# Constants multiplied into a free PSUM bank wherever the order's plan has TensorE idle

## The chip, the cores and the metric

The kernel runs on one core of a Trainium2 chip. The metric is the device time of one execution in microseconds. Before the change three runs took 1372.06, 1376.14 and 1377.72 us, a median of 1376.14 us. A fourth execution was profiled; everything said of the inside of the kernel is from it.

## The reference

One step of a streaming encoder of two layers, in fp32. There are 512 frames of a new stream (prompt) and 64 frames of a running one (sample), with D = 1024. Per layer, cut to what matters:

```python
proj = x @ w_in                      # q | k | v | conv_a | conv_gate
q, k = rope(q), rope(k)              # 8 sub heads of 64
s = q @ k.T * HEAD_DIM ** -0.5       # chunk mask in the prompt; cached keys in the sample
a = softmax(s)[0] - lam * softmax(s)[1]          # differential attention, 4 heads
o = rms_norm(a @ v) * sub_g * (1 - lam_init)
u = conv_a * sigmoid(conv_gate)
c = silu(layer_norm(depthwise_conv31(u)))
x = layer_norm(ALPHA * x + concat(o, c) @ w_out)
x = layer_norm(ALPHA * x + square(relu(x @ w_ff1)) @ w_ff2)
```

It returns x of both streams and the new keys, values and convolution states.

## The kernel before, in words

All activations lie transposed, features on the 128 partitions and the 576 frames (512 + 64) along the free dimension, in two column groups of 288 (`GS`). Eight tiles `r` of 128 features hold x. Every large product is split: an fp32 operand becomes a high half (rounded to fp32r: `wh`, and the first tile of a pair `x`) and a low half (what is left: `wl`, and the second of the pair), and `tri` multiplies three times, high by high, high by low, low by high (lines 734 to 736). The halves are made on the core: a weight block of 128 x 1024 comes by DMA into `raw`, ScalarE casts the high half (L891), VectorE or GpSimd subtracts for the low half (L894); some low halves are made by a DMA that adds (L878). The feed-forward products use a Strassen form on 2 x 2 blocks, whose sums of weight blocks and of results add work on VectorE.

The stages of a layer are: the input projection, mixed with attention and the depthwise convolution (31 taps, most of them fused multiply-adds on VectorE into PSUM, L1337); the output projection; a LayerNorm; the two feed-forward products; a second LayerNorm. In a LayerNorm the mean over features is a product with a constant matrix `ones_d` of 1/1024 (L1029 and L1034), VectorE subtracts it (L1052), ScalarE squares (L1058), GpSimd adds the squares (L1064), TensorE sums them with products that are one column wide (L1006), VectorE makes the reciprocal root (L959 to L987), TensorE spreads it (L1125), and VectorE multiplies (L1133).

PSUM is four one-bank tiles `b` and two two-bank tiles `sc`. In the rows of the order below the four `b` are called b_114 to b_117, since buffers are numbered through.

What sets the order is a planner (`Sched`). Each operation is a node with a cost in us per engine that may run it, the nodes it depends on, buffers that it acquires and releases, and a priority. `Sched.run` goes through a modelled time: an engine that is free takes the first available node by priority whose buffers are free; the instruction is issued at that moment, so each engine's program is the order in which the plan started its nodes. The plan has a model of TensorE's clock: it sums TensorE's activity in windows of 4096/1200 us (`HAMW`, `act`), and in a window after too little of it (`HAML`, `HAMH`) it doubles TensorE's costs (`cold`). Priorities and choices stand in tables of numbers, one per stage (`PHASES`); the change leaves them alone. Each engine executes its own program strictly as planned; waits on other engines are semaphores, added where tiles are written and read. So if an operation is late on the chip, what stands behind it on its engine is late too.

The lines touched are the class `Sched` (its `run`, and what decides when an engine is idle) and one helper beside `tri`.

Of the kernel before, what the change touches and what calls it, by code (L numbers as in the profile page):

```python
# [119 lines left out]
HAMW, HAML, HAMH = 4096 / 1200, 0.45, 0.9  # L120
# [13 lines left out]
GAPP = [int(i) for i in "".split()]  # L134
HB = 0
PRE = 20
PD = 0.1
DM, GD, GDL = 0.0, 0.88, 6.5
PRP, PRS = 889.2, -10.4
# [372 lines left out]
class Sched:  # L512
# [4 lines left out]
    def __init__(self, caps):  # L517
        self.free, self.nodes = {t: list(range(k)) for t, k in caps.items()}, []
        self.free["half"] = []
        self.now = None  # L520

    def room(self, tag):
# [35 lines left out]
    def delay(a, b):  # L558
# [3 lines left out]
            return 0.0  # L562
        return 0.2 if "P" in (a, b) else 0.13

    def run(self, engines):
        for n in self.nodes:
            n.left = len(n.deps)
# [8 lines left out]
        for n in reversed(order):  # L576
            n.at = min(n.eng.values()) + n.lat + max((s.at for s in n.succ), default=0.0)
            n.pri += n.at
        avail = sorted((n for n in self.nodes if n.left == 0), key=lambda n: -n.pri)
        busy = {e: 0.0 for e in engines}  # L580
        ends, t, count = [], 0.0, 0
        act, cold, win = {}, True, 0
        port = 0.0
        while count < len(self.nodes):
            again = True
            while again:
                again = False
                for e in engines:
                    if busy[e] > t + 1e-9:
                        continue  # L590
                    for i, n in enumerate(avail):
                        if n.ready > t + 1e-9 or e not in n.eng:
                            continue
                        c = n.eng[e]
# [23 lines left out]
                            n.got.setdefault(a, []).append(self.get(a))  # L618
                        self.now = {a: list(k) for a, k in n.got.items()}
                        del avail[i]  # L620
                        busy[e], n.at = t + c, t
                        if shared:
                            port = t + c
                        if e == "P":
                            a = t
                            while a < t + c - 1e-9:
                                k = int(a / HAMW + 1e-9)
                                b = min(t + c, (k + 1) * HAMW)
                                act[k] = act.get(k, 0.0) + b - a
                                a = b  # L630
# [15 lines left out]
                        break  # L646
            times = [b for b in (*busy.values(), port) if b > t] + [n.ready for n in avail if n.ready > t] + [x for x, _ in ends]
            assert times, ("stuck", count, len(self.nodes), self.free, [(n.acq, n.fn) for n in avail[:10]])
            t = min(times)
            for x, rel in [y for y in ends if y[0] <= t + 1e-9]:  # L650
                for a, n in rel:
# [10 lines left out]
def tile_hymba_step(ctx: ExitStack, tc: tile.TileContext, xT, wu, ck, cconv, par, cst,  # L662
# [29 lines left out]
    tl = {}  # L692
# [27 lines left out]
    sch = Sched(CAPS)  # L720
# [12 lines left out]
    def tri(o, wh, wl, xh, xl, start, stop):  # L733
        TE.matmul(o, wh, xh, start=start, stop=False)  # L734
        TE.matmul(o, wh, xl, start=False, stop=False)  # L735
        TE.matmul(o, wl, xh, start=False, stop=stop)  # L736

    def bank():
        return take("b")
# [1689 lines left out]
```

## Time and profile before

| what | value |
|---|---|
| median of three runs | 1376.14 us |
| the profiled execution | 1375.67 us |
| its span, first to last instruction | 1373.9 us |
| TensorE busy | 1308.0 us, 95% of the span |
| VectorE busy | 1078.1 us, 78% |
| ScalarE busy | 705.1 us, 51% |
| GpSimd busy | 302.3 us, 22% |
| mean granted TensorE clock | 0.977 of full speed |

How to read it: PE is TensorE's matmuls, PEld its weight loads (which overlap), DVE VectorE, ACT ScalarE, POOL GpSimd, SP the queue that starts most transfers. A row of a timeline has the start, the duration, the engine, the source line, the operation, output and inputs by name, and in brackets how long the engine idled before and what ended that. A row of stretches has the time from and to, its length, then busy time and number of instructions per engine in the order of its first row, then the granted clock, the share of the DMA engines and GB/s. Matmuls are pipelined: the end of one is modelled and overlaps the next, so the price of one is read from the distance of two starts. Before the first record of the clock, at 10.2 us, it is shown as 1.00. An fp32 product that isn't split stands as two records.

### The profile page before, as it was taken

The numbers are of one execution on the slowest core, as the hardware profiler recorded it, in microseconds if no ns is written. First come the engines' busy times: TensorE is split into PE (matmuls) and PEld (weight loads), VectorE is DVE, ScalarE is ACT, GpSimd is POOL, SyncE is SP. The second block draws the span as 40 slices with busy tenths as digits, with TensorE's granted clock in tenths as the row PEclk, the third lists the DMA queues.
The fourth block names the chain that finished last, engine by engine and source line by source line (L and its number), as shares of the span: only waits on it lengthen the run. The fifth ranks groups of instructions, "written<-read, shape, count | busy, mean of one in ns | idle before, by whom it ended". The sixth has DMA issues, their size and how long they took to land.

```text
span 1373.9 us, 24858 instructions
## 1 busy us (share of the span) xinstructions
PE 1308.0 (95%) x9518; PEld 1264.1 (92%) x9518; DVE 1078.1 (78%) x2206; ACT 705.1 (51%) x1413; POOL 302.3 (22%) x292
## 2 busy tenths in 40 slices
PE   8989989979999999999999999899989999999997
PEld 7878879979899999999998988798889999999996
DVE  5899998777888887878658999868677676767737
ACT  5766677265444444434156657754654443434424
POOL 0456620150000000000144885223400000000013
PEclk9999989989999999999999999899999999999998
DMA  6635533334465645554345444454234343435262
GB/s 220 162 94 140 122 117 106 93 130 156 144 211 165 208 168 192 185 167 139 102 158 204 160 152 121 129 135 118 64 79 117 112 108 108 124 80 144 70 152 69
DMA packets 70102, 186.38 MB, mean 136 GB/s; under 512 B 10848, under 2 KB 16608, under 8 KB 69984
## 3 DMA queue, kind: packets, MB, share of 16 engines
q1 hardware_dynamic: 63504, 161.20, 34.9%
q0 software_dynamic: 6480, 23.60, 10.4%
q8 instruction: 75, 1.23, 0.4%
q14 instruction: 43, 0.35, 0.1%
HBM read 154.11 MB, written 30.65 MB: 134 GB/s over the span
## 4 chain that ended last, share of the span: by engine, by line
PE 72%; DVE 18%; issue 3%; DMA 2%; ACT 2%; POOL 2%; SPq 0%; ACTq 0%; DVEq 0%; POOLq 0%
PE b L734 21%; PE b L735 21%; PE b L736 21%; DVE sc L1337 8%; DMA raw<-in_wu_dram 2%; PE sc L734 1%; PE b L1006 1%; POOL sq L1064 1%; PE sc L736 1%; PE b L1568 1%; PE sc L735 1%; DVE nm L1486 1%; DVE P L1530 1%; DMA wl<-in_wu_dram 1%; PE b L1611 1%
## 5 line engine op out<-in xcount | busy, mean ns | idle before, releaser
L734 PE MATMUL b<-x,wh 128*128 128x288 f32 x1356 | 416.2, 307 | 6.6 <-ACT wh L891 4.0
L736 PE MATMUL b<-x,wl 128*128 128x288 f32 x1356 | 406.1, 299 | 7.0 <-DVE wl L894 4.8
L735 PE MATMUL b<-x,wh 128*128 128x288 f32 x1356 | 406.5, 300 | 1.7 <-DVE x L1215 1.1
L734 PE MATMUL b<-a,wh 128*128 128x288 f32 x1088 | 325.0, 299 | 0.2 <-ACT x L731 0.2
L735 PE MATMUL b<-a,wh 128*128 128x288 f32 x1088 | 321.3, 295 | 0.0
L736 PE MATMUL b<-a,wl 128*128 128x288 f32 x1088 | 321.0, 295 | 0.0
L734 PEld LDWEIGHTS b<-x,wh 128*128 128x128 f32 x1356 | 260.5, 192 | 13.5 <-ACT wh L891 4.0
L736 PEld LDWEIGHTS b<-x,wl 128*128 128x128 f32 x1356 | 260.2, 192 | 8.2 <-DVE wl L894 5.3
L735 PEld LDWEIGHTS b<-x,wh 128*128 128x128 f32 x1356 | 260.6, 192 | 4.0 <-DVE x L1215 2.5
L734 PEld LDWEIGHTS b<-a,wh 128*128 128x128 f32 x1088 | 205.1, 188 | 2.0 <-issue 0.6
L735 PEld LDWEIGHTS b<-a,wh 128*128 128x128 f32 x1088 | 205.4, 189 | 0.5
L736 PEld LDWEIGHTS b<-a,wl 128*128 128x128 f32 x1088 | 205.1, 188 | 0.0
L2273 DVE TENSOR_TENSOR r<-r,b 128x288 f32<-128x288 f32 x192 | 85.7, 450 | 87.6 <-PE b L736 87.3
L1337 DVE SCALAR_TENSOR_TENSOR sc<-ub,par,sc 128x606 f32<-128x606 f32 x160 | 136.2, 851 | 4.2
L878 POOL DMA_DIRECT2D wl<-in_wu_dram x45 | 39.2, 871 | 446.8 <-ACT wl L875 387.6
L1064 POOL TENSOR_TENSOR sq<-sq,sq 128x288 f32<-128x288 f32 x40 | 35.7, 910 | 416.1 <-ACT sq L1058 415.5
L1325 POOL TENSOR_TENSOR r<-r,prod 128x606 f32<-128x606 f32 x72 | 113.7, 1580 | 54.8 <-ACT prod L1322 31.0
L891 ACT CAST wh<-raw 128x1024 fp32r<-128x1024 f32 (+1 forms) x73 | 71.4, 979 | 71.2 <-PE b L735 52.3
L2056 ACT CAST wh<-ckv 128x512 fp32r<-128x512 f32 x104 | 64.1, 620 | 76.7 <-PE b L735 61.2
L894 DVE TENSOR_TENSOR wl<-raw,wh 128x1024 fp32r<-128x1024 f32 (+1 forms) x73 | 84.5, 1161 | 22.3 <-ACT wh L891 21.7
L1884 DVE TENSOR_TENSOR wl<-ckv,wh 128x512 fp32r<-128x512 f32 x104 | 71.1, 685 | 6.0 <-ACT wh L2056 5.8
L875 ACT ACTIVATE wl<-raw 128x1024 fp32r<-128x1024 f32 x45 | 47.7, 1060 | 44.2 <-PE b L736 25.5
(320 smaller groups left out, 2409.9 us busy)
## 6 DMA issues: line engine op xcount, KB each, us to landing
raw<-in_wu_dram SPq DMA_DIRECT2D x110, 512.0 KB, 4.6
wl<-in_wu_dram POOLq DMA_DIRECT2D x45, 512.0 KB, 7.2
wscr<-cs SPq DMA_DIRECT2D x80, 256.0 KB, 2.0
ckv<-in_wu_dram SPq DMA_DIRECT2D x26, 512.0 KB, 3.6
ah<-in_wu_dram SPq DMA_DIRECT2D x26, 512.0 KB, 4.4
cs<-in_wu_dram SPq DMA_DIRECT2D x40, 256.0 KB, 2.8
wh<-wscr SPq DMA_DIRECT2D x20, 512.0 KB, 3.3
wl<-wscr SPq DMA_DIRECT2D x20, 512.0 KB, 4.4
```

Source lines behind the costliest of these rows:

```text
L734: TE.matmul(o, wh, xh, start=start, stop=False)
L735: TE.matmul(o, wh, xl, start=False, stop=False)
L736: TE.matmul(o, wl, xh, start=False, stop=stop)
L875: S.activation(wt["lo"], wt["raw"], AF.Copy, scale=-1.0)
L891: S.copy(wt["hi"][:, c], wt["raw"][:, c])
L894: e.tensor_tensor(wt["lo"][:, c], wt["raw"][:, c], wt["hi"][:, c].bitcast(F32), op=ALU.subtract)
L1064: e.tensor_tensor(q[a]["t"], q[a]["t"], q[b]["t"], op=ALU.add)
L1325: GP.tensor_tensor(cc[t], cc[t], st[j], op=ALU.add)
L1337: V.scalar_tensor_tensor(st["a0"], win(j), w, st["a0"], op0=ALU.mult, op1=ALU.add)
L1884: e.tensor_tensor(o, a, b, op=ALU.subtract)
L2056: S.copy(tl["wh"][box["i"]][:, off:off + n], src())
L2273: V.tensor_tensor(rr, rr, bk(), op=ALU.add)
```

## The change

When the plan has nothing that TensorE can start, and a bank `b` is free, and real TensorE work is still left, the planner now inserts a node of 0.23 us on TensorE: a product of the constant tile `ones_d` (128 x 128, fp32) with itself into the first 128 columns of the free bank. Nobody reads the result; the bank stays free in the plan, and whoever takes it next starts its accumulation anew. The node counts as activity in the plan's clock model and occupies TensorE in modelled time, so a real node that becomes available meanwhile is started up to 0.23 us later, and every later choice of the plan may differ. The limit `FT * FW` = 2.2 us on activity within the last 2.0 us is never reached. The name *keeper* is used below for such a product; the program has 129 of them.

```diff
--- before.py
+++ after.py
@@ -134,6 +134,7 @@
 GAPP = [int(i) for i in "".split()]
 HB = 0
 PRE = 20
+FT, FW, FC = 1.1, 2.0, 0.23
 PD = 0.1
 DM, GD, GDL = 0.0, 0.88, 6.5
 PRP, PRS = 889.2, -10.4
@@ -517,6 +518,7 @@
     def __init__(self, caps):
         self.free, self.nodes = {t: list(range(k)) for t, k in caps.items()}, []
         self.free["half"] = []
+        self.keep, self.recent, self.plast = None, [], None
         self.now = None
 
     def room(self, tag):
@@ -561,6 +563,19 @@
         if "N" in (a, b):
             return 0.0
         return 0.2 if "P" in (a, b) else 0.13
+
+    def spare(self, t, busy, avail):
+
+
+        if not FT or self.keep is None or busy > t + 1e-9 or not self.free["b"] or not self.left_p():
+            return False
+        return sum(min(b, t) - max(a, t - FW) for a, b in self.recent if b > t - FW) < FT * FW
+
+    def left_p(self):
+
+        while self.plast and self.plast[-1].at is not None and self.plast[-1] in self.done:
+            self.plast.pop()
+        return bool(self.plast)
 
     def run(self, engines):
         for n in self.nodes:
@@ -577,6 +592,7 @@
             n.at = min(n.eng.values()) + n.lat + max((s.at for s in n.succ), default=0.0)
             n.pri += n.at
         avail = sorted((n for n in self.nodes if n.left == 0), key=lambda n: -n.pri)
+        self.plast, self.done = [n for n in self.nodes if "P" in n.eng], set()
         busy = {e: 0.0 for e in engines}
         ends, t, count = [], 0.0, 0
         act, cold, win = {}, True, 0
@@ -618,10 +634,13 @@
                             n.got.setdefault(a, []).append(self.get(a))
                         self.now = {a: list(k) for a, k in n.got.items()}
                         del avail[i]
+                        if e == "P":
+                            self.done.add(n)
                         busy[e], n.at = t + c, t
                         if shared:
                             port = t + c
                         if e == "P":
+                            self.recent = [x for x in self.recent if x[1] > t - FW] + [(t, t + c)]
                             a = t
                             while a < t + c - 1e-9:
                                 k = int(a / HAMW + 1e-9)
@@ -646,6 +665,20 @@
                         break
             times = [b for b in (*busy.values(), port) if b > t] + [n.ready for n in avail if n.ready > t] + [x for x, _ in ends]
             assert times, ("stuck", count, len(self.nodes), self.free, [(n.acq, n.fn) for n in avail[:10]])
+            if self.spare(t, busy["P"], avail):
+                n = self.op({"P": FC}, lambda e: self.keep(e, self.free["b"][0]))
+                n.left, n.at, self.now = 0, t, {}
+                busy["P"] = t + FC
+                self.recent = [x for x in self.recent if x[1] > t - FW] + [(t, t + FC)]
+                a = t
+                while a < t + FC - 1e-9:
+                    k = int(a / HAMW + 1e-9)
+                    b = min(t + FC, (k + 1) * HAMW)
+                    act[k] = act.get(k, 0.0) + b - a
+                    a = b
+                n.fn(engines["P"])
+                count += 1
+                continue
             t = min(times)
             for x, rel in [y for y in ends if y[0] <= t + 1e-9]:
                 for a, n in rel:
@@ -734,6 +767,10 @@
         TE.matmul(o, wh, xh, start=start, stop=False)
         TE.matmul(o, wh, xl, start=False, stop=False)
         TE.matmul(o, wl, xh, start=False, stop=stop)
+
+    def keep(e, k):
+        TE.matmul(tl["b"][k][:, :128], ones_d, ones_d, start=True, stop=True)
+    sch.keep = keep
 
     def bank():
         return take("b")
```

Line numbers behind the diff's places are 33 to 37 higher in the changed kernel: `tri` is at lines 767 to 769 there, and the keeper at 772.

**At the start**, TensorE's program was, from its first product on (accumulating in b_114):

```order
L734 MATMUL b_114<-x_171,wh_83 128x288
L735 MATMUL b_114<-x_172,wh_83 128x288
L736 MATMUL b_114<-x_171,wl_87 128x288
L734 MATMUL b_114<-x_173,wh_83 128x288
L735 MATMUL b_114<-x_174,wh_83 128x288
L736 MATMUL b_114<-x_173,wl_87 128x288
```

Now it is, with keepers (L772) into the bank of the first product and then into the next free one:

```order
L772 MATMUL b_114<-ones_d 128x128 x19
L767 MATMUL b_114<-x_171,wh_83 128x288
L768 MATMUL b_114<-x_172,wh_83 128x288
L769 MATMUL b_114<-x_171,wl_87 128x288
L772 MATMUL b_115<-ones_d 128x128
L767 MATMUL b_114<-x_173,wh_83 128x288
L768 MATMUL b_114<-x_174,wh_83 128x288
L769 MATMUL b_114<-x_173,wl_87 128x288
L772 MATMUL b_115<-ones_d 128x128 x2
```

Nineteen keepers stand ahead of all real work, and single ones or pairs between the triples of products.

**Late in layer 0's attention**, TensorE's program was, around the transposes of the probabilities P (L1539), scores of the sample (`ckh`, `ckl`: cached keys), P times V (L1568) and transposes of v (L1410):

```order
L736 MATMUL sc_118<-ckh_2061,a_1832 128x512
L734 MATMUL b_114<-a_1908,a_1831 128x64
L735 MATMUL b_114<-a_1909,a_1831 128x64
L736 MATMUL b_114<-a_1908,a_1832 128x64
L1568 MATMUL b_115<-ah_99,a_1808 128x256
L1568 MATMUL b_115<-ah_99,a_1808 128x128
L1539 MATMUL b_117<-ident,P_2088 128x128 x3
L1410 MATMUL sc_119<-ident,r_98 128x128 x5
L1725 MATMUL sc_119<-dg_2127,ones_68 128x288 x2
```

Where these operations meet now (L1576, L1605 and L1447 are the same three lines), the program reads:

```order
L772 MATMUL b_117<-ones_d 128x128 x2
L1576 MATMUL b_117<-ident,P_2056 128x128
L772 MATMUL b_114<-ones_d 128x128 x2
L1576 MATMUL b_114<-ident,P_2083 128x128 x2
L772 MATMUL b_115<-ones_d 128x128 x7
L1605 MATMUL b_115<-ah_99,a_1841 128x256
L1605 MATMUL b_115<-ah_99,a_1841 128x128
L772 MATMUL b_117<-ones_d 128x128 x2
L1447 MATMUL sc_119<-ident,r_91 128x128 x5
L772 MATMUL b_117<-ones_d 128x128 x4
L767 MATMUL sc_118<-ckh_2092,a_1871 128x512
```

Seventeen keepers in five runs stand between ten real products; the scores with cached keys, which stood ahead of the first P times V, follow behind.

**In layer 0's first LayerNorm**, on VectorE, from the last multiplication of the first column group (L1133) through the subtractions of the mean in the second (L1052) to the low halves of the first feed-forward weights (L894):

```order
L1133 TENSOR_TENSOR r_91<-r_91,b_114 128x288
L1052 TENSOR_TENSOR r_97<-r_97,b_115 128x288
L1052 TENSOR_TENSOR r_95<-r_95,b_115 128x288
L1052 TENSOR_TENSOR r_98<-r_98,b_115 128x288
L1052 TENSOR_TENSOR r_94<-r_94,b_115 128x288
L1052 TENSOR_TENSOR r_92<-r_92,b_115 128x288
L819 TENSOR_TENSOR cs_3006<-cs_3006 128x512
L1052 TENSOR_TENSOR r_93<-r_93,b_115 128x288
L1052 TENSOR_TENSOR r_96<-r_96,b_115 128x288
L1052 TENSOR_TENSOR r_91<-r_91,b_115 128x288
L894 TENSOR_TENSOR wl_87<-raw_81,wh_83 128x1024
L894 TENSOR_TENSOR wl_88<-raw_82,wh_84 128x1024
```

Now (L1170, L1089 and L931 are the same lines):

```order
L1170 TENSOR_TENSOR r_98<-r_98,b_116 128x288
L931 TENSOR_TENSOR wl_87<-raw_82,wh_83 128x1024
L1089 TENSOR_TENSOR r_97<-r_97,b_114 128x288
L1089 TENSOR_TENSOR r_91<-r_91,b_114 128x288
L1089 TENSOR_TENSOR r_96<-r_96,b_114 128x288
L1089 TENSOR_TENSOR r_93<-r_93,b_114 128x288
L1089 TENSOR_TENSOR r_92<-r_92,b_114 128x288
L1089 TENSOR_TENSOR r_94<-r_94,b_114 128x288
L1089 TENSOR_TENSOR r_95<-r_95,b_114 128x288
L1089 TENSOR_TENSOR r_98<-r_98,b_114 128x288
L856 TENSOR_TENSOR cs_3056<-cs_3056 128x512
L931 TENSOR_TENSOR wl_88<-raw_81,wh_84 128x1024
```

The low half of the first weight (wl_87) moved from behind the eight subtractions to ahead of them.

On TensorE, at the same place, from the mean of the second column group (L1029, L1034) to the sums of squares (L1006), `x` being the operands of the feed-forward that the first group has already given:

```order
L734 MATMUL b_117<-x_2987,wh_83 128x288
L735 MATMUL b_117<-x_2988,wh_83 128x288
L736 MATMUL b_117<-x_2987,wl_87 128x288
L734 MATMUL b_117<-x_3001,wh_83 128x288
L735 MATMUL b_117<-x_3002,wh_83 128x288
L736 MATMUL b_117<-x_3001,wl_87 128x288
L734 MATMUL b_116<-x_2987,wh_84 128x288
L735 MATMUL b_116<-x_2988,wh_84 128x288
L736 MATMUL b_116<-x_2987,wl_88 128x288
L734 MATMUL b_116<-x_3001,wh_84 128x288
L735 MATMUL b_116<-x_3002,wh_84 128x288
L736 MATMUL b_116<-x_3001,wl_88 128x288
```

Directly behind these twelve products came L1006. Now the piece begins, with keepers around the mean (L1066, L1071):

```order
L772 MATMUL b_114<-ones_d 128x128 x8
L1066 MATMUL b_114<-sg_108,ones_d 128x288
L1071 MATMUL b_114<-r_98,ones_d 128x288
L772 MATMUL b_115<-ones_d 128x128 x7
L767 MATMUL b_115<-x_3036,wh_83 128x288
L768 MATMUL b_115<-x_3037,wh_83 128x288
L769 MATMUL b_115<-x_3036,wl_87 128x288
```

and goes on, where the first weight's products end and the second's begin:

```order
L767 MATMUL b_115<-x_3084,wh_83 128x288
L768 MATMUL b_115<-x_3085,wh_83 128x288
L769 MATMUL b_115<-x_3084,wl_87 128x288
L772 MATMUL b_117<-ones_d 128x128 x13
L767 MATMUL b_117<-x_3036,wh_84 128x288
L768 MATMUL b_117<-x_3037,wh_84 128x288
L769 MATMUL b_117<-x_3036,wl_88 128x288
```

Forty-five products and twenty keepers, seven and thirteen, now stand between the mean and the sums; eight more stand ahead of the mean. From the second unit of the feed-forward on, TensorE's order of both layers' feed-forward is what it was, with other bank numbers.

On VectorE the whole program has 2199 instructions where it had 2192, and up to the first subtraction of layer 0's LayerNorm 425 where it had 424; ScalarE has 1314 where it had 1319, GpSimd 294 where it had 297.

## The prediction

> **What bounds the kernel now.** I read the page first, then TensorE's busy time and granted clock by stretch, then its waits and the timeline at the longest of them.
>
> ```profile
> span 1373.9 us, 24858 instructions
> PE 1308.0 (95%) x9518; PEld 1264.1 (92%) x9518; DVE 1078.1 (78%) x2206; ACT 705.1 (51%) x1413; POOL 302.3 (22%) x292
> PEclk9999989989999999999999999899999999999998
> PE 72%; DVE 18%; issue 3%; DMA 2%; ACT 2%; POOL 2%; SPq 0%; ACTq 0%; DVEq 0%; POOLq 0%
> core 0: 1373.9 us, clock 0.977
> ```
>
> TensorE is busy 1308.0 of 1373.9 us, so it idles 65.9 us, and the chain that ends last runs 72% through it. The mean clock of 0.977 says that 0.023 x 1373.9 = 31.6 us of full-speed clock were missing; where it was missing it stood at a half, so some 63 us ran at half clock. The stretches show where.
>
> ```profile
> core 0: us, PE busy (x) PEld busy (x) DVE busy (x) ACT busy (x) POOL busy (x), PEclk, DMA share, GB/s
> 48.10:55.00 6.90, 6.90 (x42) 6.46 (x42) 6.62 (x11) 6.70 (x15) 5.79 (x5) 0.78 0.40 69
> 190.00:200.00 10.00, 6.56 (x31) 4.10 (x30) 9.00 (x29) 8.85 (x26) 0.88 (x1) 0.90 0.48 120
> 197.90:208.20 10.30, 9.45 (x37) 7.12 (x37) 8.36 (x18) 7.41 (x18) 3.47 (x3) 0.50 0.60 198
> 276.40:297.00 20.60, 13.07 (x59) 11.77 (x58) 13.82 (x32) 12.37 (x27) 13.99 (x15) 0.67 0.42 143
> 297.00:336.40 39.40, 39.40 (x297) 39.29 (x296) 32.01 (x58) 25.14 (x54) 7.00 (x8) 1.00 0.46 152
> 343.00:686.00 343.00, 339.77 (x2558) 338.45 (x2559) 277.75 (x563) 140.41 (x253) 4.29 (x5) 1.00 0.51 168
> 824.30:858.70 34.40, 32.32 (x234) 29.10 (x235) 32.82 (x59) 27.16 (x65) 18.42 (x13) 0.97 0.49 121
> 1020.00:1339.00 319.00, 318.38 (x2405) 318.31 (x2406) 222.00 (x460) 136.98 (x236) 14.67 (x17) 1.00 0.42 113
> ```
>
> Two stretches of feed-forward (343 to 686 and 1020 to 1339) are TensorE work without a break at full clock: 662 us where nothing can be won by a keeper. Attention (row 824.30) is as much VectorE's: 32.82 of 34.40 us. The first LayerNorm of layer 0 (276.4 to 297.0) holds 7.5 us of idle TensorE and a clock of 0.67; right behind it TensorE is the bound (39.40 of 39.40). So time saved in that LayerNorm is time saved in the end, while in attention a faster TensorE helps only where VectorE waits for it.
>
> **The price of a keeper.** A keeper is one fp32 product of 128 columns. The nearest row is P times V: three products of 256 columns and one of 128, 896 in all.
>
> ```profile
> 175.58 1.68 PE L1568 MATMUL b<-ah,a 128*128 128x256 f32 x8
> 177.01 0.38 PE L734 MATMUL b<-x,wh 128*128 128x288 f32 x1
> ```
>
> They hold TensorE from 175.58 to 177.01, 1.43 us, so 128 columns cost 1.43 x 128/896 = 0.20 us at full clock, and 0.41 at half. The order has 129 keepers: 26 us, if none fell into idle time. Thirty stand in the first 55 real products, 18 in layer 0's input projection and attention, 29 in its first LayerNorm and 8 soon behind it, 2 in its feed-forward, 10 around its last LayerNorm, 4 in layer 1's attention, 12 in its first LayerNorm and 16 at the end. A keeper also waits until its bank's last reader is done; in most places the real product behind it writes the same bank and would wait as long, so that wait I cost at nothing.
>
> **The start** (30 keepers, 19 of them ahead of everything).
>
> ```profile
> 0.74 0.20 POOL L684 MEMSET ones_d<- 128x128 f32 x1 [0.29 <-POOLq L2410]
> 9.60 0.44 PE L736 MATMUL b<-x,wl 128*128 128x288 f32 x1
> 9.84 0.44 PE L734 MATMUL b<-x,wh 128*128 128x288 f32 x1
> 10.53 0.29 PE L735 MATMUL b<-x,wh 128*128 128x288 f32 x1
> 10.66 0.29 PE L736 MATMUL b<-x,wl 128*128 128x288 f32 x1
> 16.28 0.29 PE L734 MATMUL b<-x,wh 128*128 128x288 f32 x1
> 20.12 0.40 PE L735 MATMUL b<-x,wh 128*128 128x288 f32 x1 [0.90 <-DVE x L1215]
> ```
>
> The distance of two products falls from 0.24 us (9.60 to 9.84) to 0.13 (10.53 to 10.66): the half clock of the start ends near 10.2. The 55th product begins at 16.28. Keepers can begin once the constants stand, near 1.1, and 19 of them end between 1.1 + 19 x 0.20 = 4.9 and 1.1 + 19 x 0.41 = 8.9. Fifty-five products at 0.13 and 11 keepers at 0.20 take 9.4 us more: 14.3 to 18.3, against 16.4. What is late is taken up by the wait of 0.90 us for operands at 20.12. Bounds 0 and +1.6; I take **+0.2**.
>
> **The first LayerNorm of layer 0** (the largest term).
>
> ```profile
> 278.64 0.75 PE L1029 MATMUL b<-sg,ones_d 128*128 128x288 f32 x2 [1.41 <-POOL sg L1835]
> 279.91 1.91 DVE L1052 TENSOR_TENSOR r<-r,b 128x288 f32<-128x288 f32 x5
> 282.07 7.19 POOL L1064 TENSOR_TENSOR sq<-sq,sq 128x288 f32<-128x288 f32 x6 [0.46 <-ACT sq L1058]
> 282.35 1.17 DVE L1052 TENSOR_TENSOR r<-r,b 128x288 f32<-128x288 f32 x3
> 281.74 0.68 DVE L819 TENSOR_TENSOR cs<-cs 128x512 fp32r<-128x512 f32 x1
> 283.44 3.21 DVE L894 TENSOR_TENSOR wl<-raw,wh 128x1024 fp32r<-128x1024 f32 x2
> 284.97 0.61 PE L736 MATMUL b<-x,wl 128*128 128x288 f32 x1 [4.83 <-DVE wl L894]
> 289.31 2.08 PE L1006 MATMUL b<-ones_c,sq 128*96 128x1 f32 x12 [1.28 <-POOL sq L1064]
> 292.85 0.45 DVE L987 SCALAR_TENSOR_TENSOR dg<-ident,lry 96x288 f32<-96x288 f32 x1
> 297.05 0.65 PE L1125 MATMUL b<-dg,ones 96*128 96x288 f32 x2
> ```
>
> TensorE's third product of the feed-forward waits 4.83 us, because VectorE makes the weights' low half (L894) only after eight subtractions; the clock then falls to a half, the variance sums (L1006) follow at 289.31, and the factor's broadcast (L1125) stands behind 24 products at half clock, at 297.05. The order shows two things changed: the low half of the first weight is now ahead of the subtractions, and 45 products with 20 keepers stand between mean and sums, where 12 products stood.
> By the same durations: 8 keepers take the place of the 1.41 us wait (+0.2); 7 keepers reach 281.1, when the low half (279.91 + about 1.4) is there; 15 products, 2.0 us, to 283.5; 13 keepers, 2.6, to 286.1; the second low half comes at 281.3 + 3.1 + 0.7 + 1.6 = 286.7, which covers those 13; 30 products, 4.0, to 290.7. POOL's additions shift by the 1.4 us that the subtractions are later and end at 290.7 too. Sums at full clock take 1.0, half of 2.08; the factor (L987) ended 2.0 us after them and does so again, while 18 products, 2.4 us, pass: L1125 near 294.1, so 2.9 us earlier, with 27 more products done (27 x 0.133 = 3.6). From 6.5 us go 8 keepers that follow while TensorE is full, 1.6: **-4.9**. Should the clock stay at a half, 45 + 18 products take 15.1 instead of 8.4 and 13 keepers 5.3 instead of 2.6, and L1125 comes 6.7 late: with the 3.6 and the 1.6, +4.7. Bounds -6.5 and +4.7; I take the first reading, since the 4.83 us stall that let the clock fall is gone.
>
> **Attention of layer 0.** Seventeen keepers, 3.4 us, stand in a run of transposes where only ten real products follow each other; in 190 to 200 TensorE idled 10.00 - 6.56 = 3.4 us, so they fit. The gain would be the clock: 197.9 to 208.2 ran at 0.50 with TensorE 9.45 us busy, and full speed would return at most 4.7 us; VectorE, 9.00 of 10 us busy just before, leaves less. Bounds -4.7 and +3.4; **-2.0**. VectorE's work up to the LayerNorm has one instruction more than before, so the reordered attention itself I cost at nothing, covered by VectorE's own run.
>
> **The rest.**
>
> ```profile
> 690.47 0.75 PE L1034 MATMUL b<-r,ones_d 128*128 128x288 f32 x2 [0.63 <-DVE r L2300]
> 697.00:700.40 3.40, 3.28 (x32) 3.20 (x31) 0.77 (x5) 0.70 (x3) 2.63 (x4) 0.89 0.02 5
> 700.40:703.80 3.40, 3.40 (x18) 3.40 (x18) 0.88 (x5) 0.00 (x0) 0.00 (x0) 0.60 0.00 0
> 955.40:958.80 3.40, 1.96 (x7) 1.19 (x8) 3.40 (x11) 3.40 (x8) 2.04 (x3) 1.00 0.58 117
> 965.60:969.00 3.40, 2.50 (x20) 2.27 (x18) 3.05 (x8) 0.00 (x0) 2.11 (x3) 1.00 0.00 0
> 1362.20:1365.60 3.40, 3.16 (x6) 1.22 (x5) 2.67 (x12) 1.71 (x4) 1.05 (x2) 0.55 0.64 220
> ```
>
> Layer 0's last LayerNorm with the 2 keepers in the feed-forward: 12, 2.4 us, of which a wait of 0.63 takes some, against a clock of 0.60 at 700: **+0.7** (0 to +2.4). Layer 1's attention: 4 keepers, 0.8 us, and seven more VectorE instructions in the program where VectorE is full: **+1.0** (0 to +3.0). Its first LayerNorm: 12 keepers, 2.4 us, in gaps of 1.44 and 0.90 and smaller ones: **+0.3** (0 to +2.4). The end: 16 keepers, 3.2 us, most of them in waits of the last chain, whose clock was 0.55: **+0.4** (-1.4 to +2.0).
>
> **The sum**: 0.2 - 2.0 - 4.9 + 0.7 + 1.0 + 0.3 + 0.4 = -4.3 us. The profiled execution took 1375.67 us (1.8 around its span), half a microsecond under the median of 1376.14; I predict 1371.4.
>
> **The rivals.**
> *The clock is held wherever keepers stand.* Then attention gives 4.7, the LayerNorm 6.5, the last two places 0.7 and 1.4: 13.3 us, 1362.4. For it: both stretches named follow idle TensorE, 3.4 us of it from 190 on. Against it: 48.10 to 55.00 and others have no keeper, and VectorE bounds attention.
> *Keepers stand in front of ready work.* Their number is fixed in TensorE's order and they run whether or not TensorE is late; at half clock each costs 0.41. If the clock stays at 0.50 behind the first LayerNorm, the upper bounds come together: 1.6 + 3.4 + 4.7 + 2.4 + 3.0 + 2.4 + 2.0 = 19.5; two thirds of it, since a few will meet a wait, +13.0: 1388.7. It decides from the point where the product behind the 13 keepers is ready before them. For it: the long gaps of the trace (4.83 for a low half) come where VectorE is late, which a fixed count can't follow.
> *Keepers buy no clock.* Then the LayerNorm keeps its -4.9 from the earlier low half, attention costs half its 3.4, +1.7, layer 0's last LayerNorm 2.4 - 0.63, +1.8, the end +0.9: with 0.2, 1.0 and 0.3, +1.0, 1376.7. For it: from 697 to 700.4 TensorE reads busy for 3.28 of 3.40 us, with narrow sums, and the clock is 0.60 right behind, so being busy isn't enough. Against it: keepers are 128 columns wide and not one, and the half clock at 197.9 follows a stretch that was a third idle.
> [...]
>
> **How the numbers follow.** The sum as worked out 0.40 (1365 to 1378), clock held 0.25 (1356 to 1368), ready work 0.22 (1381 to 1395), no clock 0.13 (1373 to 1380). Half a per cent, 6.9 us, is about what can be told from no change here: faster is under 1368.8. Faster: 0.25 and 0.12 of the likeliest, 0.37. Slower: 0.22 and 0.02 of the others, 0.24. Same: 0.39. The range from 1358 to 1388 leaves a tenth on each side.
>
> **What would show it.** Right: no wait for L894's successor at the first feed-forward products; a clock near 1.00 from 277 to 297; the factor's broadcast some 3 us earlier against the mean; feed-forward stretches of the same length. Wrong: 0.50 in that stretch, keepers of 0.41 us without idle behind them, or an attention of layer 0 that ends later than before by more than 3 us, because the reordering and not the keepers decides.

## The result: slower by 0.8 per cent

The changed kernel takes 1384.92 us (median of 6 runs, 1382.95 to 1389.62); the kernel before took 1374.06 us beside it (median of 6, 1371.61 to 1377.72). The ratio is 1.0082, interval 1.0066 to 1.0098: about 11 us slower, where 1371.4 us was predicted. The direction was missed; the time lies inside the predicted range.

The page of the changed kernel, with the row of its mean clock:

```profile
span 1387.7 us, 25386 instructions
PE 1336.4 (96%) x9776; PEld 1298.3 (94%) x9776; DVE 1083.6 (78%) x2213; ACT 703.9 (51%) x1408; POOL 296.5 (21%) x289
PEclk9999899999999999999999999799999999999998
core 0: 1387.7 us, clock 0.974
L772 PE MATMUL b<-ones_d x258: 270/275/582, 1.0 to 1379.0; 128*128 128x128 f32 x129
```

The 129 keepers stand as 258 records of L772. TensorE idles 1387.7 - 1336.4 = 51.3 us in place of 65.9, so they do fill idle time. The mean clock of this execution is no higher, 0.974 against 0.977, but it is the lowest, and this the slowest, of the six: the other five had 0.979 to 0.984, where the kernel before had 0.968 to 0.980 in the 63 executions beside the experiments. So in most executions the keepers did raise the clock, and the time was lost all the same. New line numbers are the old ones plus 33, and plus 37 behind `keep`: L769 is the old L736, L931 the old L894, L1066 the old L1029, L1162 the old L1125.

The profiled execution took 1389.62 us, 4.7 above the median, so the differences below add up to 13.8 us (but for the last digit), not 11. The boundaries are the starts of the products on the lines of the mean (L1029, L1066) and of the broadcast (L1125, L1162). The first and the last mean, before and after, stand in the groups of these lines:

```profile
L1029 PE MATMUL b<-sg,ones_d x12: 404/406/510, 262.8 to 1341.8; 128*128 128x288 f32 x12
```

```profile
L1066 PE MATMUL b<-sg,ones_d x12: 403/406/510, 272.7 to 1354.4; 128*128 128x288 f32 x12
```

| stretch | before, us | after, us | difference | forecast |
|---|---|---|---|---|
| start, to the 217th product | 40.6 | 39.7 | -0.9 | +0.2 |
| rest of layer 0's attention and output projection, to the first mean | 222.3 | 233.0 | **+10.7** | **-2.0** |
| first LayerNorm, to its last broadcast | 34.2 | 31.5 | -2.7 | -4.9, with the next row |
| feed-forward, to the second mean | 376.4 | 377.1 | +0.7 | |
| layer 0's last LayerNorm | 30.6 | 29.1 | -1.5 | +0.7, two keepers of the feed-forward in it |
| layer 1's attention | 232.7 | 237.2 | +4.5 | +1.0 |
| layer 1's first LayerNorm | 32.1 | 33.8 | +1.7 | +0.3 |
| layer 1's feed-forward | 372.6 | 372.7 | +0.1 | 0 |
| the end | 32.4 | 33.6 | +1.3 | +0.4 |

Most of it is layer 0's attention. Rows by stretch of the changed kernel: attention; the first and the last but one of its six stretches at half clock, 37.5 us together; the LayerNorm; the feed-forward.

```profile
0.00:272.60 272.60, 252.21 (x1752) 238.24 (x1753) 227.78 (x430) 168.99 (x357) 91.01 (x86) 0.93 0.50 133
43.66:50.49 6.83, 6.06 (x26) 5.94 (x27) 6.62 (x11) 4.22 (x7) 2.07 (x2) 0.50 0.43 127
193.85:197.26 3.41, 3.41 (x16) 3.41 (x16) 3.27 (x9) 0.97 (x3) 1.29 (x1) 0.50 0.00 0
272.60:304.10 31.50, 31.36 (x247) 30.59 (x246) 26.43 (x66) 18.22 (x38) 20.76 (x22) 1.00 0.26 85
304.10:681.20 377.10, 371.03 (x2781) 368.49 (x2780) 305.10 (x606) 161.97 (x300) 7.37 (x8) 1.00 0.50 166
```

The same stretches of the kernel before; in its attention the half clock held five times, for 23.9 us together, the first shown here and the longest, from 197.90, in the prediction.

```profile
0.00:262.80 262.80, 239.27 (x1656) 222.68 (x1657) 222.72 (x429) 168.85 (x356) 95.21 (x88) 0.95 0.51 138
47.74:51.15 3.41, 3.41 (x16) 3.41 (x15) 3.34 (x7) 3.41 (x6) 2.10 (x3) 0.50 0.05 10
262.80:297.10 34.30, 26.77 (x163) 25.15 (x162) 26.10 (x66) 18.36 (x38) 19.89 (x22) 0.80 0.26 87
297.10:673.50 376.40, 371.44 (x2788) 369.56 (x2788) 304.90 (x602) 164.49 (x304) 7.00 (x8) 1.00 0.50 166
```

Three things are to be read here. In attention TensorE idles 20.4 us instead of 23.5, but runs 13.7 us longer at half clock. In the LayerNorm the forecast came true: idle 7.5 us fell to 0.1, the clock rose from 0.80 to 1.00, and the stretch is 2.7 us shorter. And VectorE in attention is busy 227.78 instead of 222.72 us and idles 44.8 instead of 40.1: it is not a full engine that sets this time.

TensorE and VectorE of the changed kernel in that LayerNorm show each of its steps:

```profile
287.15 1.95 PE L772 MATMUL b<-ones_d 128*128 128x128 f32 x16
288.93 0.65 PE L1066 MATMUL b<-sg,ones_d 128*128 128x288 f32 x2
289.91 1.72 PE L772 MATMUL b<-ones_d 128*128 128x128 f32 x14
293.45 3.06 PE L772 MATMUL b<-ones_d 128*128 128x128 f32 x26
300.72 1.10 PE L1043 MATMUL b<-ones_c,sq 128*96 128x1 f32 x12
304.14 0.65 PE L1162 MATMUL b<-dg,ones 96*128 96x288 f32 x2
307.29 0.49 PE L772 MATMUL b<-ones_d 128*128 128x128 f32 x2 [1.31 <-ACT sgm L2054]
```

```profile
289.92 1.37 DVE L931 TENSOR_TENSOR wl<-raw,wh 128x1024 fp32r<-128x1024 f32 x1
291.21 1.90 DVE L1089 TENSOR_TENSOR r<-r,b 128x288 f32<-128x288 f32 x5
```

The low half (L931) runs ahead of the subtractions, its product no longer waits, 13 keepers take 296.27 - 293.45 = 2.8 us, the sums run at full clock (1.10 us instead of 2.08), and the broadcast follows the second group's mean by 304.14 - 288.93 = 15.2 us, where it took 297.05 - 278.64 = 18.4.

### The profile page after: what moved, and what is told of

Its sections match the earlier page's. It is cut to its first block, busy times and chain, and to the rows that moved or that the text cites. A ratio compares the mean times of both kernels' runs of the same rounds, so it can differ in the third digit from the quotient of the medians.

```text
span 1387.7 us, 25386 instructions
## 1 busy us (share of the span) xinstructions
PE 1336.4 (96%) x9776; PEld 1298.3 (94%) x9776; DVE 1083.6 (78%) x2213; ACT 703.9 (51%) x1408; POOL 296.5 (21%) x289
## 4 chain that ended last, share of the span: by engine, by line
PE 67%; DVE 13%; issue 3%; DMA 3%; ACT 2%; POOL 2%; ACTq 0%; SPq 0%; POOLq 0%; DVEq 0%
PE b L767 20%; PE b L769 19%; PE b L768 19%; DVE sc L1374 5%; PE sc L767 1%; DMA wscr<-cs 1%; PE sc L769 1%; PE b L1043 1%; PE sc L768 1%; POOL sq L1101 1%; PE b L1605 1%; DMA cs<-in_wu_dram 1%; PE b L772 1%; DVE nm L1523 1%; ACT r L1178 1%
## 5 line engine op out<-in xcount | busy, mean ns | idle before, releaser
L769 PE MATMUL b<-x,wl 128*128 128x288 f32 x1356 | 403.5, 298 | 0.1
L769 PE MATMUL b<-a,wl 128*128 128x288 f32 x1088 | 323.2, 297 | 0.0
L769 PEld LDWEIGHTS b<-x,wl 128*128 128x128 f32 x1356 | 258.2, 190 | 0.6 <-DVE wl L931 0.4
L769 PEld LDWEIGHTS b<-a,wl 128*128 128x128 f32 x1088 | 207.4, 191 | 0.0
L1101 POOL TENSOR_TENSOR sq<-sq,sq 128x288 f32<-128x288 f32 x40 | 35.7, 911 | 416.4 <-ACT sq L1095 415.8
L931 DVE TENSOR_TENSOR wl<-raw,wh 128x1024 fp32r<-128x1024 f32 (+1 forms) x73 | 84.0, 1153 | 22.5 <-ACT wh L928 21.8
```

The costliest lines, as they stand in the source:

```text
L931: e.tensor_tensor(wt["lo"][:, c], wt["raw"][:, c], wt["hi"][:, c].bitcast(F32), op=ALU.subtract)
L1101: e.tensor_tensor(q[a]["t"], q[a]["t"], q[b]["t"], op=ALU.add)
```

## The experiments

Two things could cost the time in attention: the keepers, or the order that the plan chose once it had made room for them. Of the two theories of the first four runs, A is the order and B the keepers in front of ready work. Ratios are to the kernel before, on the same chip; the column on the first mean is from one profiled execution each, where the kernel before has 262.8 us.

| run | TensorE's order in layer 0's attention | keepers in the whole program | median, us | ratio [95%] | first mean |
|---|---|---|---|---|---|
| changed kernel | new | 129 | 1384.92 | 1.0082 [1.0066, 1.0098] | +9.8 |
| e1_order_only | as changed | 0 | 1387.47 | 1.0107 [1.0083, 1.0131] | +12.8 |
| e2_old_order | as before | 46 | 1373.89 | 1.001 [0.9986, 1.0033] | -3.1 |
| e3_start | a third | 30 | 1401.61 | 1.0212 [1.0188, 1.0236] | +24.2 |
| e4_from_ln | as before | 81 | 1375.24 | 1.001 [0.9993, 1.0027] | -0.1 |
| e5_one_slot | a fourth | 0 | 1384.94 | 1.0085 [1.0056, 1.0114] | +9.8 |
| e6_ln0_only | as before | 30 | 1375.19 | 1.0017 [0.9997, 1.0037] | -1.1 |
| e7_both | as before | 72 | 1372.86 | 0.9991 [0.997, 1.0013] | -1.7 |
| e8_old_double | as before | 78 | 1375.03 | 1.0006 [0.9988, 1.0025] | -1.5 |
| e9_slot_005 | a fifth | 0 | 1383.10 | 1.0053 [1.0034, 1.0072] | +6.5 |
| e10_slot_060 | a sixth | 0 | 1386.53 | 1.0088 [1.0068, 1.0108] | +3.0 |

### The new order without keepers, and keepers without the new order

The first run plans every keeper as the change does, and issues none:

```diff
     def keep(e, k):
-        TE.matmul(tl["b"][k][:, :128], ones_d, ones_d, start=True, stop=True)
+        return
```

> The changed kernel's order to the row on every engine, but the 129 keepers are not issued (nothing else is left out). Theory A, that the new order of layer 0's and layer 1's attention loses the time and the keepers themselves cost little: 1381 to 1387 us against some 1374 of before, with the first mean of layer 0's LayerNorm again near 272 us in place of 263. Theory B, that keepers stand in front of ready work: 1372 to 1377 us, and that mean near 264.

It is as slow as the changed kernel, 1387.47 us. Its row for attention, and the longest of its six stretches at half clock:

```profile
0.00:275.60 275.60, 248.45 (x1656) 230.88 (x1657) 227.77 (x430) 169.12 (x357) 91.05 (x86) 0.91 0.49 131
203.46:220.53 17.07, 14.62 (x48) 9.86 (x47) 12.84 (x29) 10.41 (x28) 3.47 (x3) 0.50 0.53 154
```

TensorE idles 27.2 us, 3.6 more than before. At half clock it was busy 42.3 us over the six stretches, 23.0 over the five of before, which lost another (42.3 - 23.0) / 2 = 9.6 us. The two make 13.2 us, where the first mean is 12.8 late. So the order alone brings the whole loss, and in this execution more than two thirds of it, up to the first mean, is clock. Theory A held (1381 to 1387 and a mean near 272 were expected, a little too low), B fell. The keepers add clock to this order, they do not cost it: 0.968 to 0.973 in the six executions without them, 0.974 to 0.984 with them.

The second run leaves the plan as before and issues a keeper for each 0.23 us in which that plan has TensorE idle and a bank free:

```diff
             if self.spare(t, busy["P"], avail):
-                n = self.op({"P": FC}, lambda e: self.keep(e, self.free["b"][0]))
-                n.left, n.at, self.now = 0, t, {}
-                busy["P"] = t + FC
...
+                for _ in range(int((min(times) - max(t, fill)) / FC + 1e-9)):
+                    self.keep(engines["P"], self.free["b"][0])
+                    fill = max(t, fill) + FC
```

> The order of before on every engine, and keepers issued where the old plan has TensorE idle for 0.23 us or a multiple, without being planned (46 of them, 14 at the start, 13 in layer 0's attention, 6 in its first LayerNorm). Theory A: within 2 us of before, 1372 to 1376, since the order is the old one; the 4.8 us wait for the low half in the LayerNorm stays. Theory B: 46 keepers at 0.2 to 0.4 us in front of ready work, 1380 to 1388.

The 46 keepers cost nothing that could be told, 1.001 [0.9986, 1.0033], as theory A has it. In the profiled execution they did what the change is for; where the kernel before stood at 0.50 from 197.92 on, there is now

```profile
196.00:206.00 10.00, 9.47 (x64) 7.64 (x65) 9.55 (x22) 9.18 (x26) 2.95 (x3) 1.00 0.79 238
198.57 1.06 PE L763 MATMUL b<-ones_d 128*128 128x128 f32 x8
```

a clock of 1.00, and the first mean is 3.1 us early. Up to the first mean the mean clock is 0.95 before and in the two runs of this order without keepers in this attention (from the LayerNorm on, LayerNorm alone), and 0.97, 0.97 and 0.96 in the three with keepers there (this one, both, doubled). The median has none of that gain to show.

### Which part of the plan

Two runs let the plan have its keepers only in its first 20 us, or (`228 <= t`) only from layer 0's first LayerNorm on:

```diff
     def spare(self, t, busy, avail):
+        if not 0 <= t < 20:
+            return False
```

> Keepers are planned only in the first 20 us of the plan: 30 of them, all within the first 55 products. The order is that of before for the first 216 products and differs behind them, in attention. Theory A: the attention of layer 0 is lost from there, 1378 to 1386 us, with the first LayerNorm's mean 4 to 10 us later than 263. Theory B: 30 keepers at the start are taken up by waits for operands, 1374 to 1376.

Thirty keepers at the start are the slowest of all, 1401.61 us, though the last of them begins at 17.9 us and TensorE's first 216 products are those of before. The order from there on is as in the changed kernel up to product 727, and then a third one; the first mean comes 24.2 us late. Theory B fell, and A had the direction but not the size: 1378 to 1386 us and 4 to 10 us were expected.

> Keepers are planned only from layer 0's first LayerNorm on (81 of them); up to there the order is that of before, and the low half of the first weight again stands ahead of the subtractions. Theory A: that LayerNorm is shortened by 3 to 5 us and layer 1's attention, ordered anew, gives some 4 back: 1370 to 1376 us, with the first mean at 263. Theory B: 81 keepers in front of ready work, 1380 to 1390.

With the attention of before and 81 keepers from the LayerNorm on there is no loss. The LayerNorm and the feed-forward of that run:

```profile
262.70:294.20 31.50, 31.35 (x248) 30.59 (x247) 26.39 (x66) 18.15 (x38) 20.78 (x22) 1.00 0.26 85
294.20:670.60 376.40, 370.80 (x2781) 368.63 (x2781) 305.69 (x606) 162.94 (x300) 7.40 (x8) 1.00 0.50 167
```

The 34.2 us became 31.5 again. Theory A held in its total and B fell, though of A's two parts the gain is 2.8 us, not 3 to 5, and layer 1's attention gives 1.4 back, not 4.

### One slot, and nothing issued

If it is the order and not what is issued, then how little is enough to spoil it? The next run plans a single slot, at the first moment behind 25 us of the plan at which TensorE is idle and a bank free, and issues nothing in it. One product starts up to 0.23 us later in the plan (the slot also counts as activity in the plan's clock model), and the plan decides anew from there.

```diff
     def spare(self, t, busy, avail):
+        if t < 25 or len(self.used) >= 1:
+            return False
...
     def keep(e, k):
-        TE.matmul(tl["b"][k][:, :128], ones_d, ones_d, start=True, stop=True)
+        return
```

> One slot of 0.23 us is planned on TensorE, at the first idle moment of the plan behind the start, and no keeper is issued at all. TensorE's order is that of before for 676 products, then another up to the end of layer 0's output projection and in parts of layer 1's attention. Theory C (the order of before was picked for this plan; another order of the same work has more waits and more half clock, whatever moved it): layer 0's first mean (L1029 of before) comes 5 to 15 us later than before, with TensorE's idle time plus half of its busy time at half clock up to there above 35 us, where before has 30.0 and the changed kernel 35.7; total 1379 to 1389. Theory D (only the thirty slots at the start do harm, by delaying the first products): mean within 3 us of before, total 1371 to 1377.

1384.94 us: this slot, with no keeper in the program, costs as much as the whole change. Theory C held, D fell. (The 30.0 and 35.7 us in the expectation count from the 55th product on; counted so, the slotted kernel has 37.8.) The first instruction of VectorE that differs runs at 104.90 us. Its rows of time there, with one of GpSimd, first of the slotted kernel, then of the kernel before:

```profile
103.26 1.73 DVE L1377 SCALAR_TENSOR_TENSOR sc<-ub,par,sc 128x606 f32<-128x606 f32 x2
104.90 1.22 DVE L934 TENSOR_TENSOR wl<-raw,wh 128x1024 fp32r<-128x1024 f32 x1
106.03 0.93 DVE L1655 SCALAR_TENSOR_TENSOR ob<-ob,gs,b 128x288 f32<-128x288 f32 x2
100.77 1.29 POOL L1485 TENSOR_TENSOR ckl<-ckv,ckh 128x512 fp32r<-128x512 f32 x1
```

```profile
102.64 1.73 DVE L1337 SCALAR_TENSOR_TENSOR sc<-ub,par,sc 128x606 f32<-128x606 f32 x2
104.28 0.68 DVE L1445 TENSOR_TENSOR ckl<-ckv,ckh 128x512 fp32r<-128x512 f32 x1
104.89 0.93 DVE L1615 SCALAR_TENSOR_TENSOR ob<-ob,gs,b 128x288 f32<-128x288 f32 x2
```

The plan has given the cached keys' low half (0.68 us on VectorE) to GpSimd, where it takes 1.29; a weight's low half (1.22 us) has taken its place on VectorE, and everything behind is dealt out anew. So not only the order changes but also which engine does what. What TensorE waited for from 20 us to the first mean, as the view of waits groups it (total, times, longest), slotted kernel first:

```profile
PE b L1581 <- DVE P L1570: 4.5, 1, 4.5
PE sc L770 <- DVE r L1384: 3.0, 1, 3.0
PE b L1579 <- DVE P L1570: 2.9, 3, 1.3
PE b L1651 <- DVE ob L1655: 2.4, 2, 1.4
PE sc L770 <- ACT P L1542: 2.2, 1, 2.2
PE b L1651 <- DVE ah L767: 2.0, 1, 2.0
```

```profile
PE b L1541 <- DVE P L1530: 4.4, 1, 4.4
PE b L1539 <- DVE P L1530: 4.3, 3, 1.9
PE sc L734 <- DVE r L1344: 3.2, 1, 3.2
PE sc L734 <- ACT P L1502: 2.4, 1, 2.4
PE b L1611 <- DVE dg L987: 0.8, 1, 0.8
```

The large waits of before are all there again (softmax rows P, L1530 and L1570, and r). New are waits of the broadcasts of the attention's norm (L1651, before L1611): TensorE reaches them before VectorE has scaled the output of another head (L1655) or copied a result out of PSUM. Altogether TensorE idles 272.6 - 243.35 = 29.3 us, 5.7 more than before, and is busy 27.7 instead of 23.0 us at half clock, another 2.4: 8.1 of the 9.8 us. Why these waits arise under one order and not the other was not separated further.

### Does the loss go with the size of the slot?

The same with slots of 0.05 and 0.6 us:

```diff
-FT, FW, FC = 1.1, 2.0, 0.23
+FT, FW, FC = 1.1, 2.0, 0.05
```

> As the run with one slot and no keeper, but the slot is 0.05 us long in place of 0.23. TensorE's order is that of before for 952 products of layer 0's attention, then another up to layer 0's output projection, and in parts of layer 1's attention. Theory C (the order of before was picked, any other order of attention is worse, whatever moved it): first mean 3 to 15 us later than before, total 1377 to 1390. Rival E (the harm grows with how long the slot holds TensorE up, 9.8 us at 0.23): 2 us later, total 1374 to 1377.

> As before it, with one slot of 0.6 us; the order is that of before for 566 products. Theory C: again 3 to 15 us later at the first mean, without relation to the slot's length, total 1377 to 1390. Rival E: 2.6 times the 9.8 us of the 0.23 slot, 25 us later, total near 1400. Should one of these two runs come out at or under before, the order of before is one of several good ones, and theory C falls to: it depends on the draw.

Both runs are inside theory C's bounds, the second with 3.0 us at the first mean only just. Both orders are worse than the one of before, by 8.9 and 12.4 us of median, against 10.4 for the slot of 0.23: twelve times the slot, 1.4 times the loss. Rival E fell. The loss does not always sit at the same place. With 0.6 us the first mean is only 3.0 us late in the profile, and layer 1's attention, to the next mean of this kind, adds another 4.2.

### Keepers where the order is kept

> Keepers planned and issued only around layer 0's first LayerNorm (30); attention of layer 0 has the order of before, layer 1's end too. Theory C: the factor's broadcast 2.9 us earlier than before, as with keepers from there on (1375.24 against 1374.21), and the gain is kept to the end, as behind it little is moved: 1370 to 1373. Rival (keepers behind the broadcast give the gain back whatever follows): 1374 to 1376.

> Order of before up to layer 0's first LayerNorm with keepers that occupy nothing in the plan (as in the run that was 3.1 us ahead at the first mean), the planned keepers of the changed kernel inside that LayerNorm, unplanned ones behind it; 58 in all or a few more. Theory C: the two gains add, 3.1 at the mean and 2.9 at the broadcast, less about 1 us of keepers behind: end of the span 4 to 6 us before that of before, median 1368 to 1371. Rival (the 3.1 us at the mean were the chance of one execution, since the median there was only 0.3 us under before): 1371 to 1374.

> Order of before, with each unplanned keeper behind the start issued twice: 32 more products, 6.4 us at full clock. If keepers cost nothing because they run in waits (theory C), within 2 us of the run with single ones, 1372 to 1376, and no half clock at 197.9 us. If they stand in front of ready work, 4 to 7 us above it: 1378 to 1381.

The first of these is the run from the LayerNorm on with `228 <= t < 275`; the second issues unplanned keepers outside that stretch and planned ones in it; the third is the run with the old order, each keeper behind the start issued twice:

```diff
-                    self.keep(engines["P"], self.free["b"][0])
+                    for _ in range(2 if t >= 20 else 1):
+                        self.keep(engines["P"], self.free["b"][0])
```

Keepers doubled cost nothing measurable, as theory C has it: 1375.03 us beside 1373.89 for single ones, each within 0.3% of the kernel before. Up to the first mean the mean clock is 0.96 with doubled keepers, 0.97 with single ones and 0.95 in the kernel before; whether the half clock at 197.9 us was absent, as expected, this mean does not show. With keepers in the LayerNorm alone, its gain is in the trace (first mean 1.1 us early, broadcast 3.9, second mean 4.6), and not in the median: 1375.19, where 1370 to 1373 was expected; that is the rival's range, 1374 to 1376. The trace says where it went: from layer 0's last broadcast to layer 1's first mean the lead falls from 4.6 to 1.4 us. The order of layer 1's attention differs there too. That stretch took 232.7 us before, 232.6 and 233.2 in the two runs (old order, and doubled) that keep its order. One other order of it, the same on TensorE and VectorE in four runs (LayerNorm alone, both, start, slot of 0.6 us), took 234.9 to 236.9. But a new order isn't always slower there: that of the slots of 0.23 and 0.05 us took 231.9 and 232.8, and that of the changed kernel 237.2 with its keepers, 232.8 without them; nearly the same order took 234.1 in the run from the LayerNorm on. One execution each, so this is read from traces and not settled.

The run with both, 1372.86 us, is the fastest measured, but over the 1368 to 1371 expected of two gains that add, and in the rival's range. At 0.9991 [0.997, 1.0013] it is 12 us faster than the changed kernel and cannot be told from the one before.

## Why the prediction was wrong, point by point

**What bounds the kernel.** "In attention a faster TensorE helps only where VectorE waits for it" put VectorE in front. The runs say more. On TensorE the lateness of the new orders shows as idle time and half clock (13.2 us for 12.8 in the run without keepers, 8.1 of 9.8 with the slot). That says where the time went, not what made TensorE wait: by the view of waits of the run without keepers, results of VectorE ended 11.8 us of its idle time up to the first mean, and results of ScalarE 14.9. Nor is VectorE full: in the changed kernel it idles 44.8 us up to there, 4.7 more than before. So no engine alone sets the time.

**The price of a keeper** was about right: 0.20 us, where 13 took 2.8 us, 0.22 each. So was the thought that most of them lie in idle time: 32 more of them made no difference that could be measured.

**The start.** +0.2 was forecast. The 55th product begins at 17.64 us, inside 14.3 to 18.3 and 1.4 later than before; by the 217th the changed kernel is 0.9 us ahead (1.8 without keepers), outside the bounds of 0 and +1.6. TensorE's order is the same up to there and ScalarE's is not; what brought the 0.9 was not separated. The +1.6 doesn't follow from its own rows either: 18.3 - 16.4 - 0.90 = +1.0.

**The first LayerNorm of layer 0.** The local part was right step by step: no wait for the low half, clock 1.00, broadcast 15.2 us behind the mean against a forecast 294.1 - 278.6 = 15.5. What failed is what lies behind it, "with 27 more products done (27 x 0.133 = 3.6)". The feed-forward up to the second mean should have been 3.6 - 1.6 - 0.4 = 1.6 us shorter, the ten keepers counted, and was 0.7 longer. The run of the same order without keepers shows why, in its timeline and its row for that stretch:

```profile
311.23 0.40 PE L767 MATMUL b<-x,wh 128*128 128x288 f32 x1 [1.30 <-ACT sgm L2054]
308.10:683.80 375.70, 369.08 (x2761) 366.26 (x2760) 305.31 (x606) 162.84 (x300) 7.39 (x8) 1.00 0.50 167
```

TensorE, further ahead, runs into a bank that ScalarE has not read out yet, 1.30 us, and with keepers the keeper at 307.29 has the same wait; and 27 products fewer left it busy only 371.44 - 369.08 = 2.4 us less. The wait was hidden before by TensorE being late. To the second mean it is -2.1 us instead of -4.9.

**Attention of layer 0.** Here the prediction failed, in one sentence: "VectorE's work up to the LayerNorm has one instruction more than before, so the reordered attention itself I cost at nothing, covered by VectorE's own run." A count of instructions says nothing about the order they are in, nor about their time: with one more instruction VectorE was busy 5.1 us longer (227.78 against 222.72), and it had 40 us of idle time that could grow. The bounds, -4.7 and +3.4, held keepers and clock only, so the 10.7 us lay outside them. What the runs show in the place of nothing: the reordered attention by itself, without a keeper, brings the first mean 12.8 us later. VectorE's longer work is not the common cause, since the slotted kernel has 223.36 us of it, 0.6 more than before, and is 9.8 us late. The order of before is one on which the plan's small choices fall well, and each of five others of this attention, whatever moved it, lost 9 to 27 us of median. Whether the tables of priorities were chosen on that very order can't be seen from these runs; that all five others are worse is what they show.

**The clock in attention** was right about the place: without a new order, the run with keepers has a clock of 1.00 from 196 to 206 where the kernel before stood at 0.50 from 197.92 on, and in the profiled executions the changed kernel loses 4.8 us less to the clock in attention than the same order without keepers, (42.3 - 32.7) / 2. The gain in time, 2.6 us of median, is not beyond doubt, since the two intervals overlap.

**The rest.** Layer 1's attention, +4.5 against bounds of 0 to +3.0, holds one stretch of 17 us at half clock, told of below; the same order without keepers took 0.1 us more than before. The other terms lay within their bounds or, layer 0's last LayerNorm, 1.5 us under zero.

**The rivals.** "Keepers stand in front of ready work", 1388.7, came nearest in time and is wrong as a cause: there need be no keeper at all. That the time lies inside the predicted range is owed to this rival, and so to luck. "The clock is held" came true in part, in the LayerNorm with the new order and at 197.9 with the old, but not in the changed kernel's attention, with 37.5 us at half clock, and nothing near its 13.3 us was gained. "Keepers buy no clock" is contradicted by the rows at 196 and at 272.6, and by the mean clocks of the changed order, 0.974 to 0.984 with keepers and 0.968 to 0.973 without. The sentence in "what would show it" on an attention that ends more than 3 us late "because the reordering and not the keepers decides" names what happened; it should have been a rival with a price.

## What to carry to other kernels

Work that is added to a planner's model is an edit of the whole order behind it: cost the new order by itself, by running it with the added work left out, before asking what the added work does. Where an order rests on priorities, a shift in the plan can cost much more on the chip than its length (0.05 us in the plan, 8.9 us of median here), so filler goes in after the plan is made, into the order as it stands; here it then cost nothing, and gained nothing that could be told. And the idle time of an engine that shares a path with another is not to be counted as cover for a reordering: VectorE's 40.1 us in attention did not cover it here, the first mean came 12.8 us later.

## What the runs showed of the hardware

In the profiled executions of the kernel before and of the changed kernel, the stretches at half clock that lie inside the program lasted 3.41, 6.83, 10.24, 13.65 or 17.07 us. The same work had stretches of different length in two programs. In layer 1's attention the changed kernel and the same order without keepers have the same TensorE instructions around one wait:

```profile
887.25 0.79 PE L1578 MATMUL b<-ident,P 64*128 64x64 f32 x5 [2.47 <-DVE P L1567]
883.34:886.75 3.41, 1.44 (x15) 1.00 (x13) 3.18 (x11) 3.34 (x8) 0.00 (x0) 1.00 0.00 0
886.75:890.16 3.41, 2.91 (x14) 2.79 (x15) 3.27 (x8) 3.41 (x10) 1.40 (x1) 0.50 0.02 3
890.16:893.58 3.42, 3.42 (x18) 3.30 (x19) 2.71 (x8) 1.53 (x7) 0.27 (x1) 0.50 0.56 172
900.40:903.82 3.42, 3.42 (x16) 3.40 (x16) 1.90 (x9) 1.72 (x5) 0.00 (x0) 0.50 1.00 245
```

```profile
889.77 0.79 PE L1578 MATMUL b<-ident,P 64*128 64x64 f32 x5 [2.46 <-DVE P L1567]
886.13:889.54 3.41, 1.18 (x13) 0.84 (x12) 3.18 (x10) 3.33 (x7) 0.00 (x0) 1.00 0.03 5
889.54:892.96 3.42, 3.19 (x16) 3.07 (x17) 3.29 (x8) 3.42 (x9) 1.68 (x1) 0.50 0.11 22
892.96:896.37 3.41, 3.41 (x28) 2.95 (x28) 2.99 (x10) 2.88 (x10) 0.00 (x1) 1.00 0.76 195
```

After a wait of 2.47 us the first stays at half clock from 886.75 to 903.82, with TensorE busy 16.6 of the 17.07 us; the second, after one of 2.46 us, has 0.50 from 889.54 and the full clock again from 892.96. In the first the half clock begins 0.50 us ahead of the product behind the wait, in the second 0.23 us; whether these 0.27 us decide it, one pair does not show. As an estimate from the busy times at a clock of 0.50, the first lost 16.6 / 2 = 8.3 us there and the second 3.2 / 2 = 1.6, with the same instructions: 6.7 us between two executions through the clock alone. The six executions of the changed kernel had a mean clock of 0.974 to 0.984, and the one with the least was the slowest, 1389.62 us. The half clock began here in a wait of 2.47 us; in the kernel before, at 197.92, it began behind 3.41 us in which TensorE was busy 1.76 us, with waits of 0.80 and 0.84 us. A busy TensorE did not end it at once: in the changed kernel the rows from 890.16 on are full, 3.42 of 3.42 us, and still at 0.50.
